# A two-layer attention and retention trunk: preparation steps, bias rows, output-weight squares and projection loads put at other places of the schedule

## The chip, the cores and the metric

The kernel runs on one core of a Trainium2 chip. The metric is the device time of one execution in microseconds (us); smaller is better. The times before are the median, the lowest and the highest of three runs; the profile is of one more execution.

## The reference

Two layers act on x of 2048 tokens by 1024 channels. Each layer normalises x, projects it to eight groups of 512 columns, runs two kinds of heads on them, gates both and projects back.

```python
def hybrid_layer(x, norm_gain, w_in, w_out, rel_bias, cos, sin):
    hn = rms_norm(x, norm_gain)
    proj = hn @ w_in
    aq, ak, av, ag, rq, rk, rv, rg = jnp.split(proj, cuts, axis=-1)
    ya = chunked_rel_attention(aq, ak, av, rel_bias)   # 8 heads x 64, own chunk of 64 and 8 before it
    yr = chunkwise_retention(rq, rk, rv, cos, sin)     # 4 heads x 128, a state carried from chunk to chunk
    y = jnp.concatenate([ya * silu(ag), yr * silu(rg)], axis=-1)
    return x + y @ w_out
```

(The reshapes to heads are left out.) Attention adds a bias for each head by clipped distance and takes a softmax. Retention turns q and k by rotary phases and normalises its output head by head. After the second layer x is normalised once more. All of it is float32.

## The kernel before, in words

**Numbers.** Every float32 operand of a large product is held as two float16 tiles, an upper part and a rest, and each product is three passes of the tensor engine (PE): upper by upper, upper by rest, rest by upper. A weight section of 1024 by 128 is loaded as float32 by `load_sec`, squared and summed by `sumsq` on the scalar engine (ACT), summed over partitions by a small product (`allsum`), and from that a power of two is chosen as a scale. `convert` then makes the upper part on ACT and the rest on the vector engine (DVE). The float32 sections live in pool `w4`, which has three buffers.

**Stages.** A layer has four sections `s`, each with two attention heads and one retention head, and each section has four stages `n` of 512 tokens. A stage has two halves: `dense_T` (projections that come out transposed: queries, keys and their rotary turn) and `dense_V` (values and gates), of 12 rounds each. A round is eight products of 512 columns. The attention and retention of a stage run through the 24 rounds of the next one: `attention` makes one unit (128 queries of one head) in three rounds. In each unit `qk` computes scores, adds the bias and takes the exponential, the SP queue transposes the probabilities (`pT`, L827), and `pv` multiplies by the values two units later. `retention` (L869 products, L873 and L877 operands) goes in between. After the four sections, `wout` projects: for each token tile T of 128 it takes six rounds, in which PE multiplies the transposed, scaled y (tiles `yh`, `yl`) by the output weights, and DVE adds the result to x. It works with later tiles at the same time: y of T + 2 is squared, scaled and split, y of T + 1 is transposed.

**Order.** PE, ACT, DVE and GpSimd (POOL) execute in the order in which the program names their instructions. SyncE (SP), which issues nearly all DMAs, is ordered by a planner, except for issues that `in_turn` or `keep_in_program_order` pins: those stay in program order among themselves. So an issue that isn't pinned may go out long before the step that names it, as soon as its buffer is free.

**Background.** Preparation work is written as generators, put into a list by `push(generator, steps)`. `run` goes through a half stage round by round: it executes what `later(k, ...)` has put off by k rounds, takes one step of attention, and then pulls as many background steps as the remaining steps divided by the remaining rounds, rounded up:

```python
todo = sum(max(b[1], 0) for b in bg)
...
pull(min(-(-todo // max(left, 1)), todo))
left -= 1
```

The rounds that `run` counts on (`thirds`, which becomes `left`) need not be the rounds that there are; steps that are left over run in the next half. `prep_T` and `prep_V` prepare the input weights of the next section, `prep_O` the output weights (`go.os` is their scale), and `prep_Omax` the sum of squares that this scale comes from. `wout_first` takes the first steps of the projection for token tiles 0 and 1 ahead of `wout`: it loads their y and x (`y_load`, `x_load`), squares, scales and splits. `y_turn` transposes a split y by two DMAs into tiles that share buffers with the rotary tables. `bias_scratch` writes two heads' bias rows, repeated 128 times, to DRAM (two DMAs, pinned), and `bias_tiles` reads them back skewed, masks two corners on POOL and scales on ACT.

Of the kernel before, what the change touches and what calls it, by code (L numbers as in the profile page):

```python
# [18 lines left out]
P = 128  # L19
# [8 lines left out]
def hybrid_trunk(ctx: ExitStack, tc: tile.TileContext, x, pos, gain, gcol, w_in, w_out, rel, fgain,  # L28
# [468 lines left out]
    def prep_Omax(l, go):  # L497
        nm = f"O{l}"
        mm = b2.tile([P, 1], F32, tag="omax", name=f"omax{nm}")
        st = load_sec(w_out[l, :, 0:P], f"{nm}m0")  # L500
        for j in range(KT):
            yield
            m1 = sumsq(st, f"{nm}m{j}", None)
            if j + 1 < KT:
                st = load_sec(w_out[l, :, (j + 1) * P:(j + 2) * P], f"{nm}m{j + 1}")
            if j == 0:
                dve.tensor_copy(mm, m1)
            else:
                dve.tensor_tensor(mm, mm, m1, op=ALU.add)
        mm = lowp(mm, nm)  # L510
        for _ in range(4):
            yield
        m = allsum(mm, nm)
        sv, iv = norm_scale(m, nm)
        go.os = b2.tile([P, 1], F32, tag="o_s", name=f"o_s{l}")
        go.oi = b2.tile([P, 1], F32, tag="o_i", name=f"o_i{l}")
        dve.tensor_copy(go.os, sv)
        dve.tensor_copy(go.oi, iv)
        yield
# [87 lines left out]
    def later(k, fn):  # L607
        deferred.append([k, fn])
# [328 lines left out]
    def y_load(l, t):  # L937
        u = St()
        u.nm = f"y{l}_{t}"
        u.t = t  # L940
        if t < 8:
            u.y = w4.tile([P, D], F32, tag="w4", name=f"yy{u.nm}")
        else:
            u.y = b2.tile([P, D], F32, tag="q", name=f"yy{u.nm}")
        sp.dma_start(u.y, y_d[t])
        return u

    def x_load(l, u):
        if l + 1 == DEPTH or u.t < 12:
            f = (hT[l, 0] if l + 1 == DEPTH else hT_of(l + 1, NS - 1))[u.t // 2 % 2].rearrange("p k c -> p (k c)").bitcast(F32)  # L950
            u.x = f[:, u.t % 2 * D:(u.t % 2 + 1) * D]
        else:
            u.x = w4.tile([P, D], F32, tag="w4", name=f"xx{u.nm}")
        sp.dma_start(u.x, x[u.t * P:(u.t + 1) * P, :] if l == 0 else x_d[u.t])

    def y_squares(l, u):
        u.m = b2.tile([P, 1], F32, tag="ym", name=f"ym{u.nm}")
# [100 lines left out]
    def wout_first(l, go, us):  # L1058
        us.append(y_load(l, 0))
        x_load(l, us[0])  # L1060
        us.append(y_load(l, 1))
        u, v = us
        for fns in ((), (lambda: y_squares(l, u),), (lambda: y_scale(u, go),), (lambda: rows_hi(u.rows, u.y, u.sy),),
                    (lambda: rows_lo(u.rows, u.y, u.sy), lambda: y_squares(l, v)), (lambda: y_turn(u), lambda: y_scale(v, go)),
                    (lambda: rows_hi(v.rows, v.y, v.sy),), (lambda: rows_lo(v.rows, v.y, v.sy),)):
            yield
            for fn in fns:
                fn()
        yield

    def wout(l, go, gc, us, wT=None):

# [5 lines left out]
        for r in range(6 * NT):  # L1078
            T, i = divmod(r, 6)
            t, c = halves[r // 3]  # L1080
            u = us[t]
            if ring["att_done"] and i % 3 == 1:
                flow()
            for fn in events.pop(r, ()):
                fn()
            hurry = T + 3 == NT and not end
            if i == 0 and 0 < T < NT - 1 and (end or T + 2 < NT):
                rows_lo(us[T + 1].rows, us[T + 1].y, us[T + 1].sy)
            if (i == 1 and T + 1 < NT and (end or T + 2 < NT)) or (i == 5 and hurry):
                y_turn(us[T + 1 if i == 1 else T + 2])  # L1090
            if i == 0 and T + 2 < NT:
                us.append(y_load(l, T + 2))
            if i == 1 and T + 1 < NT:
                x_load(l, us[T + 1])
            if T + 2 < NT:
                v = us[T + 2]
                if i == 3 - hurry:
                    y_squares(l, v)
                if i == 4 - hurry:
                    y_scale(v, go)  # L1100
                if i == 5 - hurry:
                    rows_hi(v.rows, v.y, v.sy)
                    if hurry:
                        rows_lo(v.rows, v.y, v.sy)
            if i % 3 == 0:
                ps = psD.tile([P, 512], F32, tag="dense", name=f"dO{l}_{t}_{c}")
            for m in range(8 * (i % 3), 8 * (i % 3) + 8):
                kt, w = divmod(m, 3)
                h_, w_ = ((u.h, gc[c].vh), (u.h, gc[c].vl), (u.lo, gc[c].vh))[w]
                pe.matmul(ps, h_[:, kt, :], w_[:, kt, :], start=(m == 0), stop=(m == 23))  # L1110
            if i % 3 == 2:
                xs = u.x[:, c * 512:(c + 1) * 512]
                keep(dve.scalar_tensor_tensor(out=xs, in0=ps, scalar=u.sc[:, 0:1], in1=xs, op0=ALU.mult, op1=ALU.add))
                if end and t + 1 == NT:
                    final_half(t, u.x, c)
                if c == 1:
                    at = lambda k, fn, r=r: events.setdefault(r + k, []).append(fn)
                    if not end:
                        sp.dma_start(x_d[t], u.x)
                        rows = [w_[:, 2 + t % 2].rearrange("p k c -> p (k c)") for w_ in (wT.g.h, wT.g.l)]  # L1120
                        residual(l + 1, t, u.x, at, rows if t < 4 else None, 4 < t < 12 and t % 4 > 0)
                    elif t + 1 < NT:
                        final(t, u.x, at)
            yield
# [251 lines left out]
    for l in range(DEPTH):  # L1376
        gO = [Grp(), Grp()]
        go = Grp()
        for s in range(NSW):
            g = grp(l, s)  # L1380
            for n in range(NS):
# [6 lines left out]
                    st = st0  # L1388
                if n == 0 and not first:
                    bs, bt = bias_scratch(l, s), bias_tiles(l, s, g)  # L1390
                    later(1, lambda bs=bs: next(bs))
                    for k in (6, 10, 17, 21):
                        later(k, lambda bt=bt: next(bt))
                if (l, s) == (0, 0) and 0 < n < NS - 1:
                    if n == 1:
# [15 lines left out]
                        push(prep_O(l, 0, gO[0], go), 9)  # L1411
                if n == NS - 1 and s == 1 and l + 1 < DEPTH:
                    gain_load(l + 1)
                if not first:
                    run(dT, att, 10 if n == 0 else 14 if (l, s, n) == (0, 0, NS - 1) else 22 if (l, s) == (0, 0) else 24)
                if n == NS - 1 and s == NSW - 1:
                    us = []
                    push(wout_first(l, go, us), 10)
                if n == 2 and s == 2:
                    push(prep_Omax(l, go), 13)  # L1420
                if n == NS - 1:
                    if s + 1 < NSW:
                        push(prep_V(l, s + 1, grp(l, s + 1)), 23)
                    else:
                        push(prep_O(l, 1, gO[1], go), 9)
                run(dense_V(l, s, n, g, st), att, 24 if n == NS - 1 and s < NSW - 1 else 12)
                if first:
                    sp_order.__exit__(None, None, None)
# [88 lines left out]
```

## Time and profile before

| what | us |
|---|---|
| median of three runs | 2081.31 |
| lowest and highest run | 2080.66, 2084.20 |
| the profiled execution's own time | 2082.83 |
| its span, first to last instruction | 2081.1 |
| PE busy in the span | 2006.5 |
| DVE, ACT, POOL busy | 1229.8, 1139.5, 683.5 |

The mean granted clock of the tensor engine over the span is 0.991 of full speed. Each row of a view names the line of the kernel, the engine and the tiles as output<-inputs; "idle before" is the time that the engine stood still before an instruction, and the arrow names what released it. In the timeline, the number in square brackets is that idle time. In the chain of waits, a row is a start, a length and what the chain passed through. In a table of windows each row is a stretch (from:to, its length), the busy time of each engine with its number of instructions, the granted clock, the share of time in which the 16 DMA engines were busy, and GB/s. Since every window's DMA share counts packets by their start, it can pass 1.

Layer 0's sections begin near 0, 260, 470 and 678 us, its output projection near 878; layer 1's sections begin near 1072, 1270, 1477 and 1690, its projection near 1895.

### The profile page before, as it was taken

What the parts mean: (1) busy time and instruction counts of PE and PEld (TensorE: products, weight loads), DVE (VectorE), ACT (ScalarE), POOL (GpSimd) and SP (SyncE); (2) the same over time, 40 slices, a digit from 0 to 9 for tenths busy, and PEclk for the clock granted to TensorE, in tenths of its full rate; (3) what the DMA queues carried; (4) which work ended last, traced back from release to release, by engine and by line L of the source; (5) the groups of instructions that cost most, each with busy time, mean ns of one, the idle gap of its engine ahead of it and who ended that gap; (6) DMA issues with size and microseconds to landing.
All of it is one profiled execution on the core that took longest, in us unless ns stands there. A gap on an engine that the chain in (4) does not pass through costs nothing.

```text
span 2081.1 us, 39317 instructions
## 1 busy us (share of the span) xinstructions
PE 2006.5 (96%) x14014; PEld 1052.0 (51%) x14014; DVE 1229.8 (59%) x3817; ACT 1139.5 (55%) x2530; POOL 683.5 (33%) x701
## 2 busy tenths in 40 slices
PE   6988999999999999998999999999999999999998
PEld 4444545555555555544444555555555555554543
DVE  7776556566556555576653556555655565557643
ACT  7566665556565644555443546554655565446432
POOL 0244343444334434430002333444334334343100
PEclk9999999999999999999999999999999999999999
DMA  8678674547484854799765546554755776548874
GB/s 237 162 153 180 142 148 112 114 110 164 117 182 113 167 137 102 153 234 260 203 163 118 125 104 148 120 126 103 152 111 128 178 146 161 127 102 192 211 199 125
DMA packets 645701, 313.63 MB, mean 151 GB/s; under 512 B 459232, under 2 KB 602080, under 8 KB 645504
## 3 DMA queue, kind: packets, MB, share of 16 engines
q1 hardware_dynamic: 645504, 311.12, 65.5%
q8 instruction: 109, 1.79, 0.4%
q14 instruction: 88, 0.72, 0.1%
HBM read 123.26 MB, written 41.98 MB: 79 GB/s over the span
## 4 chain that ended last, share of the span: by engine, by line
PE 49%; DMA 2%; ACT 2%; DVE 1%; issue 0%; SPq 0%; POOL 0%; POOLq 0%; ACTq 0%; DVEq 0%
PE dT L748 15%; PE dV L767 14%; PE dO L1110 13%; PE r L869 2%; DMA pT<-pq 1%; PE S L816 1%; PE S L815 1%; PE o L835 1%; PE o L836 1%; PE o L837 1%; ACT stO1m L312 0%; ACT sc L822 0%; PE ptn L1011 0%; DVE sc L819 0%; ACT pq L824 0%
## 5 line engine op out<-in xcount | busy, mean ns | idle before, releaser
L825 POOL TENSOR_TENSOR pq<-sc,pq 128x640 f16<-128x640 f32 (+4 forms) x256 | 319.6, 1248 | 872.1 <-ACT pq L824 460.2
L822 ACT ACTIVATE sc<-sc,mq,cT 128x640 f32<-128x640 f32 (+4 forms) x256 | 218.4, 853 | 629.4 <-DVE rl L841 338.3
L767 PE MATMUL dV<-whV,hTh 128*128 128x512 f16 x1024 | 353.1, 381 | 4.3 <-DVE gt L785 4.2
L767 PE MATMUL dV<-wlV,hTh 128*128 128x512 f16 x1024 | 353.2, 381 | 0.0
L767 PE MATMUL dV<-whV,hTl 128*128 128x512 f16 x1024 | 353.1, 380 | 0.0
L748 PE MATMUL dT<-hTh,whT 128*128 128x512 f16 x1008 | 349.2, 382 | 2.1 <-DMA hTh<-xa 1.1
L748 PE MATMUL dT<-hTh,wlT 128*128 128x512 f16 x1008 | 348.0, 380 | 0.0
L748 PE MATMUL dT<-hTl,whT 128*128 128x512 f16 x1008 | 347.8, 380 | 0.0
L767 PEld LDWEIGHTS <-hTh 128*128 128x128 f16 x2048 | 196.8, 98 | 219.2 <-DVE gt L785 6.5
L748 PEld LDWEIGHTS <-whT 128*128 128x128 f16 x2016 | 193.0, 98 | 214.9 <-issue 10.6
L819 DVE CUSTOM_DVE_ANT_0 sc<-S,bias 128x640 f32<-128x640 f32 (+4 forms) x256 | 188.3, 736 | 112.7 <-PE S L816 111.3
L1110 PE MATMUL dO<-whO,yly 128*128 128x512 f16 x512 | 194.6, 380 | 1.5 <-DMA yly<-hTl 0.8
L1110 PE MATMUL dO<-whO,yhy 128*128 128x512 f16 x512 | 194.8, 381 | 1.0 <-DMA yhy<-hTh 1.0
L1110 PE MATMUL dO<-wlO,yhy 128*128 128x512 f16 x512 | 194.8, 380 | 0.0
L824 ACT ACTIVATE pq<-sc 128x640 f16<-128x640 f32 (+4 forms) x256 | 171.5, 670 | 8.1
L1110 PEld LDWEIGHTS <-yhy 128*128 128x128 f16 x1024 | 99.9, 98 | 116.1 <-DMA yhy<-hTh 1.5
L767 PEld LDWEIGHTS <-hTl 128*128 128x128 f16 x1024 | 99.3, 98 | 110.6 <-issue 1.9
L748 PEld LDWEIGHTS <-wlT 128*128 128x128 f16 x1008 | 97.5, 98 | 113.1 <-issue 6.2
L815 PE MATMUL S<-k,q 128*128 128x128 f16 (+3 forms) x592 | 142.9, 268 | 0.2
L835 PE MATMUL o<-v,pT 128*128 128x65 f16 x1120 | 130.0, 194 | 12.3 <-DMA pT<-pq 12.3
L836 PE MATMUL o<-v,pT 128*128 128x64 f16 x1120 | 130.2, 195 | 0.0
L816 PE MATMUL S<-k,q 128*128 128x128 f16 (+3 forms) x592 | 130.2, 268 | 0.0
(352 smaller groups left out, 3462.1 us busy)
## 6 DMA issues: line engine op xcount, KB each, us to landing
q<-qq SPq DMA_DIRECT2D x128, 128.0 KB, 2.4
yyy<-y_d SPq DMA_DIRECT2D x32, 512.0 KB, 4.7
stT<-in_w_in_dram SPq DMA_DIRECT2D x27, 512.0 KB, 5.1
stV<-in_w_in_dram SPq DMA_DIRECT2D x26, 512.0 KB, 4.7
k<-kk SPq DMA_DIRECT2D x128, 64.0 KB, 2.0
swp<-rot SPq DMA_DIRECT2D x64, 128.0 KB, 2.7
tabc<-tab SPq DMA_DIRECT2D x32, 256.0 KB, 3.0
tabs<-tab SPq DMA_DIRECT2D x32, 256.0 KB, 3.2
```

The costliest lines, as they stand in the source:

```text
L748: pe.matmul(ps, w_[:, j, kt, :], h_[:, kt, :], start=(m == 0), stop=(m == 23))
L767: pe.matmul(ps, h_[:, kt, a * P:(a + 1) * P], w_[:, kt, :], start=(m == 0), stop=(m == 23))
L815: pe.matmul(o, st.q[:, hx, 0, cs], k_, start=True, stop=False)
L816: pe.matmul(o, st.q[:, hx, 1, cs], k_, start=False, stop=True)
L819: dve.tensor_tensor_reduce(out=v, in0=S[:, 0:w], in1=g.bias[hx][:, 640 - w:640], scale=1.0, scalar=-3.0e38, op0=ALU.add, op1=ALU.max, accu ...
L822: act.activation(v, v, AF.Exp, bias=m[:, 0:1], scale=g.c[:, 0:1])
L824: act.activation(pq[:, 0:w], v, AF.Copy)
L825: pool.tensor_tensor(pq[:, w:2 * w], v, pq[:, 0:w], op=ALU.subtract)
L835: pe.matmul(o[:, 0:65], u.p[:, b, :], v_[:, 0:65], start=(b == 0), stop=False)
L836: pe.matmul(o[:, 0:64], u.p[:, b, :], v_[:, 65:129], start=False, stop=False)
L869: pe.matmul(out_, w_, m_, start=(i == 0), stop=(i + 1 == len(pairs)))
L1110: pe.matmul(ps, h_[:, kt, :], w_[:, kt, :], start=(m == 0), stop=(m == 23))
```

## The change

Five edits. (1) In the last stage of layer 0's first section, the divisor of `dense_T`'s run goes from 14 to 18, which spreads the 25 steps of section 1's `prep_T`. (2) At the start of a section, `bias_scratch` runs in the third round instead of the first, and the first two steps of `bias_tiles` in rounds 7 and 11 instead of 6 and 10. (3) `prep_Omax` is pushed before `dense_T` of stage 2 of section 2 instead of before its `dense_V`, with 21 steps instead of 13; it has two sections loaded or loading at a time. (4) `wout_first` is pushed before `dense_T` of a layer's last stage, with a divisor of 12, instead of before `dense_V`; it no longer transposes tile 0, which `with_turn` does in the eighth of its rounds beside `prep_O`. (5) y loads from tile 2 and x loads from tile 1 on are pinned, and y of tile T + 3 is loaded in round 3 of tile T instead of in round 0 of tile T + 1.

```diff
     def prep_Omax(l, go):
         nm = f"O{l}"
         mm = b2.tile([P, 1], F32, tag="omax", name=f"omax{nm}")
-        st = load_sec(w_out[l, :, 0:P], f"{nm}m0")
+        load = lambda j: load_sec(w_out[l, :, j * P:(j + 1) * P], f"{nm}m{j}")
+        for _ in range(4):
+            yield
+        sts = [load(0), load(1)]
+        for _ in range(4):
+            yield
         for j in range(KT):
             yield
-            m1 = sumsq(st, f"{nm}m{j}", None)
-            if j + 1 < KT:
-                st = load_sec(w_out[l, :, (j + 1) * P:(j + 2) * P], f"{nm}m{j + 1}")
+            m1 = sumsq(sts[j], f"{nm}m{j}", None)
+            if j + 2 < KT:
+                sts.append(load(j + 2))
...
-        sp.dma_start(u.y, y_d[t])
+        i = sp.dma_start(u.y, y_d[t])
+        if t > 1:
+            in_turn(i)
         return u
...
-        sp.dma_start(u.x, x[u.t * P:(u.t + 1) * P, :] if l == 0 else x_d[u.t])
+        i = sp.dma_start(u.x, x[u.t * P:(u.t + 1) * P, :] if l == 0 else x_d[u.t])
+        if u.t:
+            in_turn(i)
...
-                    (lambda: rows_lo(u.rows, u.y, u.sy), lambda: y_squares(l, v)), (lambda: y_turn(u), lambda: y_scale(v, go)),
+                    (lambda: rows_lo(u.rows, u.y, u.sy), lambda: y_squares(l, v)), (lambda: y_scale(v, go),),
...
+    def with_turn(gen, us):
+
+        for r in range(12):
+            if r == 7:
+                y_turn(us[0])
+            next(gen, None)
+            yield
...
-            if i == 0 and T + 2 < NT:
-                us.append(y_load(l, T + 2))
+            if r == 0 or (i == 3 and T + 3 < NT):
+                us.append(y_load(l, T + 3 if r else 2))
...
-                    later(1, lambda bs=bs: next(bs))
-                    for k in (6, 10, 17, 21):
+                    later(3, lambda bs=bs: next(bs))
+                    for k in (7, 11, 17, 21):
                         later(k, lambda bt=bt: next(bt))
...
+                if n == 2 and s == 2:
+                    push(prep_Omax(l, go), 21)
+                last = n == NS - 1 and s == NSW - 1
+                if last:
+                    us = []
+                    push(wout_first(l, go, us), 9)
                 if not first:
-                    run(dT, att, 10 if n == 0 else 14 if (l, s, n) == (0, 0, NS - 1) else 22 if (l, s) == (0, 0) else 24)
-                if n == NS - 1 and s == NSW - 1:
-                    us = []
-                    push(wout_first(l, go, us), 10)
-                if n == 2 and s == 2:
-                    push(prep_Omax(l, go), 13)
+                    run(dT, att, 12 if last else 10 if n == 0 else 18 if (l, s, n) == (0, 0, NS - 1) else 22 if (l, s) == (0, 0) else 24)
                 if n == NS - 1:
                     if s + 1 < NSW:
                         push(prep_V(l, s + 1, grp(l, s + 1)), 23)
                     else:
-                        push(prep_O(l, 1, gO[1], go), 9)
+                        push(with_turn(prep_O(l, 1, gO[1], go), us), 12)
```

## The prediction

> **What bounds the kernel now.** I read the page first, then the waits of PE, then a table of windows over the stretches that the diff touches, then single rows.
>
> ```profile
> span 2081.1 us, 39317 instructions
> ## 1 busy us (share of the span) xinstructions
> PE 2006.5 (96%) x14014; PEld 1052.0 (51%) x14014; DVE 1229.8 (59%) x3817; ACT 1139.5 (55%) x2530; POOL 683.5 (33%) x701
> ```
> PE is busy for all but 74.6 us; no other engine passes 59%. The change adds and removes no matmul, so it can win only inside those 74.6 us and in PE's clock. Who ends PE's idle time:
> ```profile
> PE o L835 <- DMA pT<-pq: 12.3, 11, 2.1
> PE r L869 <- DVE dT L877: 8.1, 9, 2.1
> PE r L869 <- DVE sh L877: 8.1, 5, 4.2
> PE msg L326 <- DVE mbg L319: 5.0, 1, 5.0
> PE r L869 <- ACT dT L873: 4.3, 3, 1.5
> ```
> Two families: the transposed probabilities (pT) arrive late from the SP queue, and retention's small products (r) come before ACT and DVE have made their operands (dT, sh). Where they lie (stretch, length, PE, PEld, DVE, ACT, POOL busy, granted clock, DMA share, GB/s):
> ```profile
> 195.00:235.00 40.00, 36.43 (x285) 19.71 (x286) 22.69 (x81) 26.38 (x57) 13.28 (x12) 1.00 0.75 169
> 1270.00:1297.00 27.00, 25.59 (x200) 13.64 (x199) 16.73 (x59) 16.38 (x39) 5.92 (x8) 1.00 0.80 188
> 1477.00:1503.00 26.00, 24.12 (x173) 12.20 (x170) 15.34 (x52) 16.01 (x37) 5.60 (x7) 0.93 0.92 193
> 570.00:595.00 25.00, 25.00 (x196) 13.61 (x194) 12.44 (x40) 12.42 (x26) 9.41 (x9) 1.00 0.69 148
> 595.00:620.00 25.00, 22.60 (x171) 11.92 (x170) 15.41 (x52) 19.25 (x47) 10.09 (x10) 1.00 0.91 217
> 1611.00:1636.00 25.00, 22.60 (x164) 11.81 (x163) 14.67 (x52) 19.14 (x46) 8.77 (x8) 0.94 0.89 223
> 849.00:878.00 29.00, 26.71 (x209) 14.53 (x207) 18.82 (x56) 18.89 (x40) 15.36 (x13) 1.00 0.61 139
> 1866.00:1895.00 29.00, 26.70 (x206) 14.48 (x205) 19.39 (x56) 18.73 (x40) 15.39 (x13) 1.00 0.67 129
> 878.00:936.00 58.00, 54.30 (x404) 28.75 (x402) 40.39 (x115) 31.17 (x61) 17.85 (x15) 0.97 1.03 231
> 936.00:980.00 44.00, 38.51 (x199) 17.87 (x198) 26.71 (x70) 23.37 (x43) 3.60 (x5) 0.96 1.11 259
> 980.00:1071.00 91.00, 91.00 (x445) 43.76 (x444) 52.57 (x110) 40.71 (x70) 4.40 (x8) 1.00 0.78 199
> 1895.00:1910.00 15.00, 13.34 (x100) 6.72 (x98) 11.35 (x36) 8.95 (x19) 3.36 (x3) 1.00 1.10 295
> 878.71:882.12 3.41, 3.41 (x23) 1.73 (x21) 1.62 (x4) 3.38 (x7) 1.40 (x1) 0.50 1.07 260
> 974.28:977.69 3.41, 3.35 (x12) 2.31 (x13) 3.20 (x14) 2.73 (x4) 0.00 (x0) 0.50 1.02 281
> 1493.11:1496.52 3.41, 3.41 (x9) 1.22 (x8) 1.47 (x8) 2.32 (x7) 0.59 (x1) 0.50 0.91 227
> 1633.05:1636.46 3.41, 3.02 (x12) 1.37 (x13) 1.80 (x8) 2.02 (x5) 0.28 (x1) 0.50 1.36 309
> 616.60:620.00 3.40, 2.49 (x20) 1.37 (x21) 2.78 (x12) 1.04 (x2) 0.55 (x1) 1.00 0.98 251
> ```
> Length less PE's busy time is what a stretch has to give. 570:595 and 980:1071 are quiet neighbours with no idle time. The last five rows come back below.
>
> **The change part by part.** The profiled execution took 2082.8 us, 1.7 more than its span and 1.5 above the median of the three timed runs (2081.3); I sum against the first and carry the difference over to the median.
>
> *(a) First preparation of section 1.* The last stage of section 0 (from 195 us) gives its 25 steps 18 divisor rounds instead of 14. Worked by the rule in run(): with 14, two steps fall in each of eleven rounds; with 18, two in each of seven rounds and then one. Square and scale of a weight section are three steps apart, so at two a round the sum on PE comes one round after the square on ACT:
> ```profile
> 218.51 0.16 PE L326 MATMUL msT<-mbT,ones 128*128 128x1 bf16 x1 [1.70 <-DVE mbT L319]
> ```
> This is the third section; the first two fall in the seven unchanged rounds and keep their share of the stretch's 3.57 us. The third gets three rounds and its 1.70 should go. The fourth section's steps slip into the projection after it, again two rounds from square to sum as before, and by its fifth round both schedules are at the same step. Gain 1.7; bounds 0 and 3.4.
>
> *(b) Bias rows.* At the start of a section with n = 0 two broadcast writes go out, now two rounds later; the first two bias-tile steps go one round later (a load, or two POOL memsets and an ACT copy), and those have a whole stage until L819 reads them, so I cost them at nothing. The writes now stand:
> ```profile
> 1273.85 1.17 SPq L567 DMA_DIRECT2D toep<-rel_d  x2
> 1275.12 0.53 SPq L297 DMA_DIRECT2D stT<-in_w_in_dram  x1
> 1276.19 4.97 SPq L827 DMA_TRANSPOSE pT<-pq  x1
> ```
> ```profile
> DMA to landing us min/median/max: 2.3/3.0/9.4
> ```
> ```profile
> 1276.19 8.93 DMA pT<-pq
> 1285.13 0.04 issue
> 1285.17 0.20 PE o L835
> ```
> The second fence is over all pT transposes, the third the chain of waits. A transpose that takes 3.0 us in the median took 8.93 behind three large transfers, and PE began its products the moment it landed. The stretch's idle time is 27.00 - 25.59 = 1.41 us here and 26.00 - 24.12 = 1.88 in the next section. Two rounds later the writes follow this transpose. The next one follows three rounds after it: an attention unit is three rounds, and the next unit's L835 starts 1291.56 - 1285.17 = 6.4 us on, so a round is 2.1 us.
> ```profile
> 1291.56 0.19 PE L835 MATMUL o<-v,pT 128*128 128x65 f16 x1
> ```
> The writes would go out near 1278, land like today's in 5 to 6.4 us, and the next transpose, issued near 1285 behind them and the q copies, has till about 1290. Its 3.0 us fit, narrowly. Gain 1.41 + 1.88 = 3.3; bounds 0 (the stall moves one unit on) and 3.3.
>
> *(c) Squares of the output weights.* Eight squares on ACT today run in the projection half of stage 2, section 2; the generator now starts with the transposed half, loads two ahead, and puts three squares there and five in the first five rounds of the other half.
> ```profile
> L312 ACT ACTIVATE stO0m<-stO0m x8: 1039/1042/1058, 595.0 to 614.2; 128x1024 f32<-128x1024 f32 x8
> ```
> ```profile
> 616.64 0.29 PE L869 MATMUL r<-rv,dT 128*128 128x128 f16 x2 [1.53 <-ACT dT L873]
> ```
> ACT is 19.25 of 25 us busy there and 12.42 of 25 just before. PE idles 2.40 us in layer 0 and 2.40 in layer 1 (595:620 and 1611:1636). Moving three squares of 1.04 us levels ACT at about 15.5 and 16.1, and the last rounds, where PE waits, have no square left. Against that: 18.89 of 29 us at 849:878 is the same share, and PE waits there too. I take 3.6 of 4.8; bounds 0 and 4.8. The loads go out earlier into a DMA share of 0.69; that hides them.
>
> *(d) First steps of the output projection.* wout_first (two squares, two scalings and two splits of y) ran with prep_O's second half in one projection phase: 19 steps in 12 rounds, two a round at first. Now its nine steps take nine of the 12 rounds before, the prep_O steps go one a round, and the transposes of the first y tile come at the eighth. ACT is left with four of its eight 128x1024 steps in 849:878. At about 1.04 us each that takes 18.89 to 14.7 of 29, the share of the quiet row 570:595. Idle: 2.29 and 2.30 us; they include a trailing 0.1 that stays. Gain 4.4; bounds 0 and 4.6. What is late next: the transposes of the first y tile, whose rows are now ready a half stage early; they need only land before the first output product.
>
> *(e) Loads of the projection pinned in program order.* y of tile T+3 is asked for three rounds earlier than before, but y and x loads may no longer be drawn ahead on SP.
> ```profile
> L945 SPq DMA_DIRECT2D yyy<-y_d x32: 319/565/1742, 751.8 to 2036.0; - x32
> ```
> ```profile
> L954 SPq DMA_DIRECT2D xxy<-in_x_dram x4: 333/459/593, 952.3 to 1051.0; - x4
> ```
> ```profile
> DVE hTh L1006 <- DMA x_d<-hTh: 5.1, 1, 5.1
> ```
> ```profile
> 974.34 0.48 PE L1011 MATMUL ptn<-ident,hTh 128*128 128x128 f32 x1 [2.31 <-DVE ymy L966]
> ```
> The x tiles 12 to 15 (xxy) are fetched from 952 us on, in a stretch with DMA share 1.11, though the projection asks for them after 1000 us, where the share is 0.78. There a store that DVE waits 5.1 us for sits in a full SP queue, and PE stands 2.31. Idle time: 3.70 (878:936), 5.49 (936:980) and 1.66 (1895:1910), together 10.85. Pinning takes loads out of 936:980 but moves no bytes away from 878:936, and layer 1's x tiles, fetched early today, come into 1895:1910. I take half, 5.4; bounds -4 and 10.8. The loads keep about six rounds before their use, more than 12 us at 2.1 a round.
>
> Waits removed: 1.7 + 3.3 + 3.6 + 4.4 + 5.4 = 18.4. New waits: the pT waits above are eleven of up to 2.1 us each; I charge two such, 4.2, for transfers that now meet another transpose. Net 14.2.
>
> *The clock.* In four of the touched places a stretch of 3.41 us at clock 0.50 begins within 3 us of a stall (878.71, 974.28, 1493.11, 1633.05), and matmul work that would take 1.7 us takes 3.4. The equal stall of 2.40 before 618 us leaves the clock at 1.00 (616.60:620.00), so where it falls decides. If two of the four go and a new wait brings one, 1.7 more. The Trainium skill (TensorE: Matmul & The Clock Gate, Part 1) says that an idle window of some 3.4 us, free-running, halves the clock, and advises against idle gaps over that length; by that rule gaps of 2.4 us cost no clock, and the sum would stay at 14.2. The rows here show halving after shorter ones, so I go by the rows.
>
> Sum: 14.2 + 1.7 = 15.9; 2082.8 - 15.9 = 2066.9, by the median **2065.4, say 2065**.
>
> **The rivals.** *Stalls move, they don't go.* The bias writes meet the next transpose, ACT's lag meets retention's product six rounds earlier, (e) gives nothing: 1.7 + 4.4 remain, 2075. For it: the narrow fit in (b), the equal ACT share in (c). The Trainium skill (DMA: Bandwidth & Descriptors, Queues, rings and completion order) has each engine consume a ring's descriptors in order, so bytes moved past one transpose stand before the next; that is this rival's mechanism, and no run here yet shows the next one late.
> *The order is not what the diff writes.* SP's unpinned issues are placed by a planner: the first y load goes out at 751.8, some 125 us before its products. If SP's order stays much as it is and the level of ACT matters less than I think: 2081, no change.
> *Slower.* In the five tiles of each layer that run beside attention, every y and x load now stands at a fixed place in SP's line, in front of a transpose that PE waits for. By (b), three large transfers cost a transpose 8.93 - 3.0 = 5.9 us, about 2.0 each; two loads by five tiles by two layers are 40 us of added latency. Without (e) the other parts gain 15.9 - 5.4 = 10.5; from the point where more than 10.5 of the 40 reaches PE the kernel is slower, and 15 give 2081.3 - 10.5 + 15 = 2086. Against: today's loads stand before transposes too, at worse places.
>
> **How the numbers follow.** About 0.2% (4.2 us) is what a measurement of this kernel can tell. Chances: forecast 0.60 (its own range 2054 to 2072), stalls move 0.17, no change 0.09, slower 0.14. Everything removed, 25.2 us and the four clock stretches, gives 2081.3 - 25.2 - 6.8 = 2049; 2053 is low enough. The upper end, 2082, takes in the first two rivals and leaves out the slower one. Faster 0.76, same 0.10, slower 0.14.
>
> **What would show it.** Right: 595:620's counterpart without idle time at its end; no 1.20 and 1.01 before the first output product; pT near 3 to 5 us at the start of sections 1 and 2 of layer 1; xxy loads after 1000 us; fewer rows at clock 0.50. Wrong: L835 waits of 2 us one unit further on; L1110 waiting for yhy or yly tile after tile; DVE L1113 waiting for an x load.

## The result, and the profile after

The changed kernel takes 2064.71 us (median of four runs, 2061.84 to 2066.02) where the kernel before takes 2080.98 (four runs, 2078.07 to 2084.20): a ratio of 0.992 [0.9901, 0.9938]. In another set of runs the same two kernels stood at 2062.35 and 2079.75, 0.9916 [0.9899, 0.9932]. The code of the changed kernel has moved a little: L827, L835, L869, L873, L877, L945, L954 and L1110 of before are L832, L840, L874, L878, L882, L950, L961 and L1127 now.

The page of the profile after (its execution took 2061.84 us, the lowest of the four):

```profile
span 2060.0 us, 39310 instructions
PE 1997.9 (97%) x14014; PEld 1049.6 (51%) x14014; DVE 1231.2 (60%) x3817; ACT 1137.7 (55%) x2530; POOL 687.9 (33%) x701
```

The same 14014 matmuls. PE (busy time, share, instructions) is idle for 62.1 us where it was 74.6, and its busy time is 8.6 us shorter with the same work: that second part can't come from waits. From the list of PE's waits after (in all us, how many, the longest):

```profile
PE r L874 <- DVE dT L882: 8.6, 11, 2.1
PE dV L772 <- DVE gt L790: 6.4, 5, 3.3
PE o L840 <- DMA pT<-pq: 6.0, 6, 2.4
```

The late transposes have halved, from 12.3 us in eleven waits to 6.0 in six. The wait on ACT's dT (4.3 in three) is gone; the wait on DVE's dT has grown from 8.1 to 8.6, and that of the projections (dV) on DVE's gate operand gt from 4.2 in two to 6.4 in five. By place (stretch, length, PE, PEld, DVE, ACT, POOL busy, granted clock, DMA share, GB/s), after:

```profile
195.00:243.00 48.00, 44.28 (x346) 24.04 (x347) 26.96 (x99) 30.91 (x67) 18.40 (x16) 1.00 0.72 160
284.00:294.00 10.00, 10.00 (x71) 5.19 (x69) 6.28 (x22) 5.72 (x15) 6.59 (x9) 1.00 0.74 152
1259.00:1286.00 27.00, 27.00 (x218) 14.63 (x216) 18.21 (x62) 17.04 (x39) 5.56 (x6) 1.00 0.89 196
1464.00:1490.00 26.00, 26.00 (x202) 14.04 (x201) 17.32 (x58) 16.46 (x38) 5.31 (x5) 1.00 0.87 199
591.00:616.00 25.00, 23.50 (x184) 12.44 (x183) 15.59 (x55) 17.66 (x42) 9.05 (x8) 1.00 0.99 216
1594.00:1619.00 25.00, 23.56 (x173) 12.24 (x172) 15.31 (x55) 17.37 (x42) 9.04 (x8) 1.00 0.95 218
843.00:872.00 29.00, 27.74 (x219) 15.37 (x218) 19.46 (x46) 17.26 (x38) 16.01 (x13) 1.00 0.83 168
1847.00:1876.00 29.00, 27.47 (x218) 15.19 (x216) 19.98 (x47) 16.78 (x37) 16.02 (x13) 1.00 0.85 161
872.00:930.00 58.00, 54.43 (x410) 28.50 (x407) 38.08 (x119) 32.17 (x62) 18.21 (x16) 1.00 0.99 209
930.00:974.00 44.00, 41.18 (x214) 19.27 (x215) 29.02 (x68) 23.86 (x46) 3.77 (x6) 0.96 1.10 256
1876.00:1891.00 15.00, 15.00 (x122) 8.06 (x121) 10.26 (x35) 9.30 (x19) 4.75 (x4) 1.00 0.83 205
932.72:936.13 3.41, 3.41 (x10) 1.24 (x9) 1.94 (x6) 2.47 (x6) 0.55 (x1) 0.50 1.23 222
```

and four stretches of before that were not shown (the last two hold a whole pair of touched places each):

```profile
195.00:243.00 48.00, 44.42 (x347) 24.14 (x348) 27.03 (x99) 30.89 (x67) 17.25 (x16) 1.00 0.70 157
284.00:294.00 10.00, 7.97 (x49) 3.80 (x47) 6.58 (x21) 4.71 (x12) 6.15 (x7) 0.88 0.99 151
849.00:975.00 126.00, 114.52 (x788) 58.45 (x786) 82.01 (x229) 68.64 (x134) 36.81 (x33) 0.98 0.96 221
1866.00:1910.00 44.00, 40.04 (x304) 21.20 (x303) 30.74 (x91) 27.68 (x59) 18.75 (x16) 1.00 0.82 186
```

Length less PE's busy time, before to after: first preparation 3.58 to 3.72; start of the sections of layer 1 1.41 and 1.88 to 0 and 0; the same place in layer 0 (284:294) 2.03 to 0; squares 2.40 and 2.40 to 1.50 and 1.44; first steps of the projection 2.29 and 2.30 to 1.26 and 1.53; projection 10.85 to 3.57 + 2.82 + 0 = 6.39. In the last row the clock is at half. It is the only such stretch after 250 us, apart from the last 4 us, which stand at half clock in both executions; before had five there, the four of the prediction and one at 291.6. Over the whole execution, that end left out, the half-clock time went from 34.0 us to 13.6.

### The profile page after: what moved, and what is told of

It reads as the page before. It is cut to its first block, busy times and chain, and to the rows that moved or that the text cites. A ratio compares the mean times of both kernels' runs of the same rounds, so it can differ in the third digit from the quotient of the medians.

```text
span 2060.0 us, 39310 instructions
## 1 busy us (share of the span) xinstructions
PE 1997.9 (97%) x14014; PEld 1049.6 (51%) x14014; DVE 1231.2 (60%) x3817; ACT 1137.7 (55%) x2530; POOL 687.9 (33%) x701
## 5 line engine op out<-in xcount | busy, mean ns | idle before, releaser
L827 ACT ACTIVATE sc<-sc,mq,cT 128x640 f32<-128x640 f32 (+4 forms) x256 | 218.4, 853 | 615.7 <-DVE rl L846 298.3
L1127 PE MATMUL dO<-whO,yly 128*128 128x512 f16 x512 | 194.7, 380 | 1.4 <-DMA yly<-hTl 1.4
L1127 PE MATMUL dO<-wlO,yhy 128*128 128x512 f16 x512 | 194.8, 380 | 0.0
L1127 PE MATMUL dO<-whO,yhy 128*128 128x512 f16 x512 | 194.7, 380 | 0.0
L1127 PEld LDWEIGHTS <-yhy 128*128 128x128 f16 x1024 | 100.0, 98 | 115.1 <-issue 1.4
L840 PE MATMUL o<-v,pT 128*128 128x65 f16 x1120 | 129.4, 193 | 6.0 <-DMA pT<-pq 6.0
```

The costliest lines, as they stand in the source:

```text
L827: act.activation(v, v, AF.Exp, bias=m[:, 0:1], scale=g.c[:, 0:1])
L840: pe.matmul(o[:, 0:65], u.p[:, b, :], v_[:, 0:65], start=(b == 0), stop=False)
```

## The experiments

The theory, T: each part works where the prediction put it, by taking a wait off PE, and the parts add up. The rivals: a stall only moves one unit or one section on; or a part gives nothing and another does its work.

**Each part alone, on the kernel before** (before: 2079.85 us in these runs).

*Bias rows alone.*

```diff
-                    later(1, lambda bs=bs: next(bs))
-                    for k in (6, 10, 17, 21):
+                    later(3, lambda bs=bs: next(bs))
+                    for k in (7, 11, 17, 21):
```

> Before with only the bias rows later. If the broadcast writes hold up the transpose behind them, PE's idle time of 1.41 us near 1285 and of 1.88 us near 1492 goes, and with the second of them the half-clock stretch at 1493: 3.3 to 5.0 us less than before, near 2077. If the 2.03 us near 291 belongs to this part as well (it is gone in the changed kernel), up to 3.7 us more (2.03 and a half-clock stretch of 1.7). Rival: the writes only meet the next transpose; L835 then waits 1 to 2 us one unit later and the time stays within 1 us of before.

Measured: 2075.81 us, 0.9984 [0.9973, 0.9994]. Its windows at the starts of section 1 of layer 0 and of sections 1 and 2 of layer 1:

```profile
284.00:294.00 10.00, 10.00 (x71) 5.24 (x70) 6.14 (x21) 5.53 (x15) 6.77 (x9) 1.00 0.72 154
1266.00:1293.00 27.00, 27.00 (x213) 14.66 (x212) 16.34 (x56) 17.58 (x43) 6.69 (x6) 1.00 0.80 183
1471.00:1497.00 26.00, 26.00 (x203) 14.04 (x202) 15.81 (x56) 17.15 (x42) 6.69 (x6) 1.00 0.85 186
```

All three stalls go with this edit alone, the one at 291 us that the prediction didn't count too. The stall doesn't come back one unit later: the next wait on a transpose in these sections is one of 0.43 us at 1506.

*Squares of the output weights alone* (the new `prep_Omax`, and its push):

```diff
+                if n == 2 and s == 2:
+                    push(prep_Omax(l, go), 21)
...
-                if n == 2 and s == 2:
-                    push(prep_Omax(l, go), 13)
```

> Before with only the squares of the output weights spread over both halves. If ACT's backlog is what PE waits for, the two stalls of 2.40 us (near 617 and 1633) shrink to the 1.2 to 1.4 us that the changed kernel shows there, and the half-clock stretch at 1633 goes: 2 to 4 us less than before, near 2078. Rival: the loads, not the squares, matter, since they fill the DMA engines near 600; then pT waits change in that place and not retention's.

Measured: 2077.20 us, 0.9991 [0.9982, 1.0]. The waits of PE between 582 and 620 us:

```profile
PE dV L772 <- DVE gt L790: 0.6, 1, 0.6
PE r L874 <- DVE dT L882: 0.6, 1, 0.6
```

The 1.53 behind ACT is gone, two waits of 0.6 on DVE are next. The idle time of the place is 1.33 here and 1.50 in the whole change, so this part stands by itself, and it gives about half of what it was after. The time alone wouldn't tell: its interval reaches 1.

*First steps of the projection alone.*

```diff
-                if n == NS - 1 and s == NSW - 1:
+                last = n == NS - 1 and s == NSW - 1
+                if last:
                     us = []
-                    push(wout_first(l, go, us), 10)
+                    push(wout_first(l, go, us), 9)
...
-                        push(prep_O(l, 1, gO[1], go), 9)
+                        push(with_turn(prep_O(l, 1, gO[1], go), us), 12)
```

(with the new `with_turn`, the shorter `wout_first` and the divisor of 12, as in the whole change).

> Before with only the first projection steps moved a half stage ahead and the first transposes of y in the eighth round. If ACT's load at the end of the last half is the cause, the stalls of 2.21 us before the first output product shrink by 0.7 to 1.0 us in each layer, and the half-clock stretch at 879 goes: 2 to 4 us less than before. Rival: the transposed y tiles that are ready earlier change the order on the SP queue, and the waits on pT and yly between 889 and 962 change as well, by more than 2 us in sum.

Measured: 2079.61 us, 0.9999 [0.999, 1.0007]: nothing.

*Pinned loads alone.*

```diff
-        sp.dma_start(u.y, y_d[t])
+        i = sp.dma_start(u.y, y_d[t])
+        if t > 1:
+            in_turn(i)
...
-            if i == 0 and T + 2 < NT:
-                us.append(y_load(l, T + 2))
+            if r == 0 or (i == 3 and T + 3 < NT):
+                us.append(y_load(l, T + 3 if r else 2))
```

(and x likewise).

> Before with only the projection's x and y loads pinned and y asked for three rounds earlier. If loads drawn ahead by the planner are what fills the SP queue, PE's idle time between 880 and 980 falls from 9.2 us to about 6.4 as in the changed kernel, layer 1's 1.67 us at 1897 and 1905 goes, and the half-clock stretch at 974 with its 2.31 us stall goes: 4 to 6 us less than before. Rival: pinning alone moves stalls from one transpose to another, and the projection keeps 8 us or more of idle time; the gain there in the changed kernel then comes from the first steps being done earlier.

Measured: 2078.71 us, 0.9992 [0.9983, 1.0001]: 1.1 us, hardly more than nothing. The four parts alone give 4.0, 2.7, 0.2 and 1.1 us, 8.1 of the 16.3, and the fifth, the first preparation, has yet to be placed. Either the first preparation is worth 8 us, or two of the parts need each other.

**The two projection parts together**, on the kernel before (2079.75 us in these runs): both edits above.

> Before with the first projection steps and the pinned loads together, nothing else. Alone the two gave a ratio of 0.9999 and 0.9992, and each alone left 9.1 us or more of PE's idle time in the two projections' first 100 us (11.4 + 2.7 us with the first steps, 7.1 + 2.7 with the loads). If they need each other (early first steps free the buffers of w4, which the planner then fills with y loads unless they are pinned), both together show about 6.4 + 0 us there, as the changed kernel does, and some 6 to 9 us less than before in time. Rival: the parts simply add, and the rest of the change's 16 us comes from elsewhere: 1 to 2 us less than before, with 9 us or more of idle time left in the projections.

Measured: 2069.30 us, 0.9949 [0.9934, 0.9965]: 10.4 us, where the two alone gave 0.2 and 1.1. Now the sum fits: 4.0 + 2.7 + 10.4 = 17.1, beside 17.4 of the whole change in this set of runs. The same places in the three kernels, first steps alone:

```profile
849.00:975.00 126.00, 114.21 (x791) 57.70 (x788) 77.87 (x211) 64.73 (x128) 37.49 (x33) 0.99 0.96 217
1866.00:1910.00 44.00, 40.00 (x299) 21.27 (x297) 27.70 (x79) 24.84 (x53) 19.20 (x16) 0.96 0.77 174
```

pinned loads alone:

```profile
849.00:975.00 126.00, 116.63 (x807) 59.67 (x806) 83.48 (x235) 70.56 (x136) 37.43 (x33) 0.99 0.93 208
1858.00:1902.00 44.00, 38.99 (x291) 20.56 (x290) 26.75 (x79) 27.36 (x58) 19.41 (x16) 0.96 0.79 164
```

and both:

```profile
849.00:975.00 126.00, 118.92 (x820) 60.64 (x818) 84.95 (x229) 71.10 (x141) 37.08 (x34) 1.00 0.97 220
1852.00:1896.00 44.00, 41.31 (x315) 22.06 (x314) 27.48 (x80) 26.12 (x57) 19.59 (x17) 1.00 0.88 176
```

Idle time of PE, the two stretches added: before 11.48 + 3.96 = 15.4, first steps alone 15.8, loads alone 14.4, both 9.8. So 5.6 us of the 10.4 are idle time here. And with both, no half-clock time falls into these stretches, where first steps alone, loads alone and before each have two such beginning in them. In the first of the two stretches the first steps alone take PE's waits on retention's operands from 2.2 us to 0.6, but its waits on pT go from 4.3 to 7.1; with both, the waits on pT are 3.4. The reason for the longest of these waits stands in SP's queue. First steps alone, the queue about 880 us, a row being the start, the time that the issue took and what was issued:

```profile
879.37 0.46 SPq L945 DMA_DIRECT2D yyy<-y_d  x1
879.92 0.38 SPq L928 DMA_DIRECT2D y_d<-yr  x1
880.39 0.38 SPq L945 DMA_DIRECT2D yyy<-y_d  x1
880.87 1.39 SPq L704 DMA_TRANSPOSE kt<-rot  x1
882.35 4.75 SPq L827 DMA_TRANSPOSE pT<-pq  x1
```

```profile
889.10 0.20 PE L835 MATMUL o<-v,pT 128*128 128x65 f16 x1 [2.80 <-DMA pT<-pq]
```

Both parts, the same place:

```profile
878.80 0.38 SPq L303 DMA_DIRECT2D stT<-in_w_in_dram  x1
879.28 1.40 SPq L704 DMA_TRANSPOSE kt<-rot  x1
880.77 0.59 SPq L850 DMA_DIRECT2D y_d<-ya  x1
881.46 1.49 SPq L827 DMA_TRANSPOSE pT<-pq  x1
```

With the first steps half a stage earlier, their float32 tiles come free half a stage earlier, and the unpinned y loads of 512 KB are drawn ahead into the free buffers: four within 11 us (869.7, 871.8, 879.4, 880.4; the kernel before has its four from 877.7 on), the last two right in front of a transpose of pT, which lands 6.70 us after it was issued at 882.35. PE waits 2.80 for it. With the loads pinned the next y load comes only at 886.4, the transpose issued at 881.46 lands after 3.53, and nobody waits. Pinning gives back what the first steps alone would lose; pinning alone has little to mend, since the buffers come free late anyway. This is read from one wait of layer 0; the others weren't followed one by one. The loads-alone kernel holds two changes, the pins and the y load three rounds earlier; which of the two matters isn't known.

**The first preparation undone**, on the changed kernel (before: 2079.40 us in these runs).

```diff
-18 if (l, s, n) == (0, 0, NS - 1)
+14 if (l, s, n) == (0, 0, NS - 1)
```

(a piece of the line with `run(dT, ...)`).

> The changed kernel with the divisor of the first preparation set back from 18 to 14. The trace of the changed kernel has lost the wait of 1.70 us at 218 but has two new ones, 0.56 at 230 and 1.25 at 241. If part (a) only moves its wait, setting it back changes the time by less than 1 us, gives the 1.70 back and takes the two new ones away. Rival: it also moved loads on the SP queue and with them the 2.03 us near 291 of the kernel before; then that wait returns, with 2 to 4 us.

Measured: 2062.97 us, 0.993 [0.9913, 0.9947], the time of the changed kernel. The first preparation is worth nothing. The changed kernel's timeline of PE shows why:

```profile
230.47 0.16 PE L326 MATMUL msT<-mbT,ones 128*128 128x1 bf16 x1 [0.56 <-DVE mbT L319]
...
241.50 0.16 PE L326 MATMUL msV<-mbV,ones 128*128 128x1 bf16 x1 [1.25 <-DVE mbV L319]
```

The 1.70 at 218.51 is gone; 0.56 at the last of the four T sections and 1.25 at the first V section have come, 1.81 in all. With the divisor set back, the 1.70 is there again (at 219.03) and these two are not.

**The squares moved further**, on the changed kernel, in two ways. All earlier by four rounds, seven of the eight in the transposed half:

```diff
-        for _ in range(4):
-            yield
         sts = [load(0), load(1)]
...
-                    push(prep_Omax(l, go), 21)
+                    push(prep_Omax(l, go), 17)
```

> The changed kernel with the squares of the output weights four rounds earlier still, so that seven of eight fall into the transposed half, where ACT is busy half of the time. If ACT's backlog in the second half is what is left of those stalls, the 1.39 us near 598 to 614 and the 1.21 us near 1610 to 1617 fall below 0.5 each: about 2 us less than the changed kernel. Rival: ACT is not short there but late by its own chain of exponentials; then the waits stay, or new ones come in the transposed half.

Measured: 2070.03 us, 0.9962 [0.9947, 0.9976], 6 to 10 us more than the other three kernels of these runs. My reason for trying it, that the fewer squares stand in the second half the better, fell. PE's timeline, and ACT's:

```profile
589.81 0.23 PE L872 MATMUL r<-rv,dT 128*128 128x128 f16 x1 [2.64 <-DVE dT L880]
```

```profile
587.94 1.06 ACT L312 ACTIVATE stO0m<-stO0m 128x1024 f32<-128x1024 f32 x1 [4.26 <-DMA stO0m<-in_w_out_dram]
```

The fault isn't ACT's busy share but its order: a square stood 4.26 us waiting for its own weights (issued at 581.98, landed at 587.91), DVE behind it waited for the square's sum, and PE for DVE. Four rounds earlier this section wasn't there yet. So, at a square a round, the three squares that the change puts in the transposed half are near what the loads allow.

Slower, a square every second round:

```diff
             yield
+            if j:
+                yield
             m1 = sumsq(sts[j], f"{nm}m{j}", None)
...
-                    push(prep_Omax(l, go), 21)
+                    push(prep_Omax(l, go), 24)
```

> The changed kernel with one square in every second round over both halves instead of one in each of eight rounds. If ACT falls behind because a square a round is more than it has room for, wherever they stand (four rounds earlier only moved the stall to 590 and 1597, with 2.4 to 2.6 us), half the rate leaves no stall above 0.5 us in these two stages: 2 to 4 us less than the changed kernel. Rival: any square that falls between retention's first product and its operand delays it; then stalls of 0.5 to 1 us appear at several places and the sum stays near 1.5 us a layer.

Measured: 2063.48 us, 0.992 [0.9905, 0.9936], as the changed kernel beside it (2062.35). Its idle time at the place is 1.52 in layer 0 and 2.26 in layer 1: no square is late, but small waits on DVE and on a transpose take their place.

**Half of the output preparation moved with the first steps**, so that `with_turn` runs a half stage earlier:

```diff
                     push(wout_first(l, go, us), 9)
+                    push(with_turn(prep_O(l, 1, gO[1], go), us), 12)
                 if not first:
-                    run(dT, att, 12 if last else
+                    run(dT, att, 24 if last else
```

(the push before `dense_V` goes, and the transposes come in the tenth of its rounds, not the eighth; the expectation names the seventh).

> The changed kernel with the second half of the output weights also started in the transposed half of the last stage, so that its last split on ACT comes three rounds earlier, and with the transposes of the first y tile in the seventh round. If the splits near the end of the half are what is left of the stall before the first output product, 1.26 us at 872 and 1.53 at 1875 fall below 0.5: about 2 us less than the changed kernel. Rival: the stall there is the chain of retention itself, and stays.

Measured: 2060.20 us, 0.9909 [0.9892, 0.9927]. Its windows:

```profile
843.00:872.00 29.00, 29.00 (x226) 15.81 (x224) 18.89 (x52) 18.68 (x40) 15.43 (x13) 1.00 0.89 195
1847.00:1876.00 29.00, 29.00 (x239) 16.24 (x237) 19.17 (x51) 17.84 (x39) 15.05 (x13) 1.00 0.85 176
```

The 1.26 and 1.53 us that the changed kernel still waits there are gone, though ACT is busier (18.68 of 29 us against 17.26). So the level of ACT wasn't what PE waited on; the wait goes with the order of the steps. DVE's rows in the changed kernel show which step it was:

```profile
869.82 1.28 DVE L336 SCALAR_TENSOR_TENSOR wlO<-stO,o_s,whO 128x1024 f16<-128x1024 f32 x1
...
871.28 0.28 DVE L882 SCALAR_TENSOR_TENSOR dT<-dT,r 128x128 f16<-128x128 f16 x1
```

The split of an output-weight section, 1.28 us on DVE, stands in front of retention's dT, which PE waits for until 871.61; in layer 1 the same split stands at 1873.58. With the preparation half a stage earlier, no split stands there: DVE makes dT at 869.37.

*The slower squares and this together.*

> The slower squares and the earlier second half of the output weights, both on the changed kernel. If they are independent, their gains add: 4 to 8 us less than the changed kernel, near 2058, with no idle time above 0.5 us in the stages with squares and in the last stage of each layer. Rival: the output weights' loads and the longer list of squares get in each other's way through the three buffers of w4, and the sum is no better than the earlier output weights alone.

Measured: 2059.09 us, 0.9901 [0.9885, 0.9916], the lowest of all. The places of the first steps hold 0.07 us or less of idle time, those of the squares 2.9 and 2.2, more than in the changed kernel. Beside the changed kernel in the same runs (0.9916 [0.9899, 0.9932]) the intervals overlap: that this version beats it by the 3 us of the medians isn't settled, and neither is the gain of the version above.

**The next section's weight loads pinned too**, on the changed kernel, for a wait of 2.45 us in its profile:

```profile
924.55 0.57 SPq L961 DMA_DIRECT2D hTh<-in_x_dram  x1
925.22 2.32 SPq L832 DMA_TRANSPOSE pT<-pq  x1
```

```profile
931.96 0.20 PE L840 MATMUL o<-v,pT 128*128 128x65 f16 x1 [2.45 <-DMA pT<-pq]
```

The transpose that PE waits for is the one issued at 925.22: it lands at 931.91, 6.69 us later. In front of it stands an x load. The loads that the expectation blames (two y tiles, a weight section and the mask) are issued from 927.60 on, behind it. In the kernel before, the same order (x load, transpose at 933.20) gave 5.27 us and a wait of 0.83.

```diff
-            sp.dma_start(st[i], v[:, i * h:(i + 1) * h, :])
+            in_turn(sp.dma_start(st[i], v[:, i * h:(i + 1) * h, :]))
```

> The changed kernel with the loads of the next layer's first weight sections pinned too, in layer 0's projection. If weights drawn ahead on the SP queue are what still delays pT there (a wait of 2.45 us at 932, behind two y tiles, a weight section and the mask, and a half-clock stretch with it), that wait goes: 2 to 4 us less than the changed kernel, with nothing lost later. Rival: the weights are then late for their squares, and the next layer's preparation or its first products wait; no gain, or up to 5 us lost near 1050.

Measured: 2064.19 us, 0.9931 [0.9914, 0.9947]: no gain. The wait shrinks to 1.34 us (at 932.97), but the idle time of the projection is 6.6 us against 6.39; other waits took its place. That the pins shrink it isn't shown either: the next profile, of the changed kernel as it is, doesn't have the 2.45.

**The changed kernel again**, as a second profile.

> The changed kernel once more, to stand beside the others on one chip: near 0.992 of before, with PE's idle time by stage within 0.7 us of its first profile after the first 200 us, and half-clock stretches at places that differ from its first profile's, if the clock's windows run free of the program.

Measured: 2062.35 us, 0.9916 [0.9899, 0.9932]. PE's idle time repeats within about 1 us (63.1 in all, 62.1 in the first), but not every wait of the projection does: the 2.45 at 931.96 isn't there, and an earlier transpose is waited for 2.11 until 916.62 (0.93 at that place in the first). The half-clock stretch after 250 us begins at 917.3 here, not at 932.7.

## Why the prediction was right, and where its steps were off

Forecast: 14.2 us of waits and 1.7 of clock. The two profiled executions differ by 21.1 us of span: 12.5 of idle time and 8.6 of PE's busy time, which goes with the clock (below). The medians differ by 16.3, since the profile of before lies 1.9 above its median and the profile after 2.9 below. So the forecast of the time held, and the make-up of the sum less well; that the total came so close is partly luck. (a), (c), (d) and (e) gave 7.0 us less than forecast, and a charge for new waits that was too high, a wait at 291 us that wasn't counted and a larger gain of clock made up for it. Of the signs named, two didn't come: the stage with the squares still waits 0.57 us near its end, and other waits took the place of the 1.20 and 1.01 before the first output product.

*(a)* 1.7 forecast, -0.1 measured, and no time lost when it is undone. The step that failed is the last: "the fourth section's steps slip into the projection after it, again two rounds from square to sum as before". They slip, but with V's steps behind them at two a round, and the waits came there. The stall moved one section on.

*(b)* 3.3 forecast; 3.3 went at the two places (0.29 came elsewhere in the second one's stage), and 2.0 more at 284:294. In layer 1 the order is as worked out, the transpose first and then the writes:

```profile
1263.01 0.38 SPq L297 DMA_DIRECT2D stT<-in_w_in_dram  x1
1265.13 1.26 SPq L832 DMA_TRANSPOSE pT<-pq  x1
1266.45 1.22 SPq L572 DMA_DIRECT2D toep<-rel_d  x2
...
1271.49 1.99 SPq L832 DMA_TRANSPOSE pT<-pq  x1
```

The transposes land in 3.0 to 5.0 us here instead of 8.93. The wait at 291 us in layer 0, which the prediction doesn't have, is another matter. The writes of that section are issued at 256.92 and 257.81 in the kernel before and have landed by 263; in front of the transpose stands a weight load:

```profile
280.44 2.38 SPq L297 DMA_DIRECT2D stT<-in_w_in_dram  x2
284.50 1.73 SPq L827 DMA_TRANSPOSE pT<-pq  x1
```

With the bias edit alone the order here is the same, but the second weight load lands after 5.03 us instead of 7.19 and the transpose after 3.98 instead of 6.24. All five profiles without the bias edit have a wait at this place (0.69 to 2.03 us), the nine with it none above 0.21. So this gain belongs to the edit, which also moves two steps of `bias_tiles` by a round, but how it comes about isn't shown.

*(c)* 3.6 forecast, 1.9 measured. The mechanism was right (the wait behind ACT's square went), the size off: with ACT levelled, DVE's operands are next (0.6 us a wait in the experiment).

*(d)* 4.4 forecast, 1.8 measured. The argument was ACT's share of the stretch, 14.7 of 29 us; it came to 17.26 and 16.78. The experiment with `prep_O` beside it has a higher share and no wait, so the share was the wrong measure: what is waited for is a split of 1.28 us on DVE, which the prediction doesn't count.

*(e)* 5.4 forecast, as half of what was there; 4.5 measured. The x tiles are fetched from 1012.8 us on, and DVE's wait of 5.1 for the store in a full queue is down to 2.1. But it is a gain of (d) and (e) together. The forecast added them as separate terms, and for (d) named the transposes as what comes late next; what came next in fact was the y loads of (e), drawn ahead into the buffers that (d) frees. That (e) would pin them is why the sum still held.

*New waits.* 4.2 charged; by these terms (-0.1 + 3.3 + 2.0 + 1.9 + 1.8 + 4.5 = 13.4) against 12.5 in all, about 0.9 came elsewhere. Of that, PE's idle time before 195 us, where no edit works, grew from 34.9 us to 36.0, with a wait of 1.60 for gt at 67.82. The wait of 2.45 at 932, 0.83 before, lies inside (e)'s 4.5.

*The clock.* 1.7 forecast, some 8 measured between the two profiles and some 4 over all runs. I let two of four stretches go and one come; all four went, that at 291.6 too, and one came at 932.7. The rest of the 20.4 us of half clock that is missing lies in the first 250 us, which the change hardly touches. Over the fourteen profiled executions, PE's busy time runs with the time at half clock, from 1996.7 us with 10.2 to 2006.5 with 34.0, and single ones lie up to 2 us off that line: 9.8 for 23.8, or 1.4 us for each stretch of 3.41. By that the 20.4 us are 8.4 of the 8.6. About half of that is the luck of these two executions: the mean granted clock is 0.9937 over the 49 runs of the kernel before that list it, and the profile of before, at 0.991, is at their lowest; over the eight runs of the changed kernel it is 0.9960. A difference of 0.0023 over some 2070 us is 9.5 us at half clock, an estimated 3.9 us of time, about what the medians leave after the idle time (16.3 - 12.5).

*The rivals.* Stalls move: true of (a), and in small of (c), not of (b). The order isn't what the diff writes: true of the first steps alone, where unpinned loads spoiled it, not of the whole. Slower by loads in front of transposes: at 932 us an x load stands in front of a late transpose, with 2.45 us of wait and a half-clock stretch behind it. But the same order was there before, with 0.83, and not every execution pays it; the price is 1.6 us, not the 15 that the rival needed.

## What to carry to other kernels

Where transfers are placed by a planner, a step that frees a buffer earlier also lets the next unpinned load out earlier: look at which transfer that is and which short one it will stand in front of, and change both together. Try the parts alone before believing that they add up; here two parts worth 0.2 and 1.1 us were worth 10.4 together. And a spread of preparation that moves one wait should be followed to the end of its list of steps, since what is spread less at the front is packed at the back.

## What the runs showed of the hardware

A wait of about 2 us of PE can cost another 1.4 us by the clock, and whether it does varies from one execution to the next. Before 195 us, where no edit works, all fourteen profiles hold the same waits, of the same or nearly the same length. After the one of 2.07 us near 95 us, a stretch of 3.41 us at half clock begins within 1.2 us in six profiles and not in the other eight; the changed kernel, profiled twice, is once among the six and once among the eight. Around the end of the wait of 2.55 us near 43 us such a stretch begins in eight of the fourteen, of the 3.26 near 185 us in ten, and of the one of 3.6 to 4.5 near 109 us in all. The two stretches at 932.7 and 917.3 each stand right behind the longest wait of their own projection (2.45 and 2.11). By the Trainium skill (TensorE: Matmul & The Clock Gate, Part 1), an idle window of some 3.4 us is what halves the clock; the waits of 2.07, 2.55 and 3.26 us named here are shorter, so the trace doesn't agree.

A transpose in SP's queue lands later behind large transfers: at nearly the same place it landed 3.53 us after its issue with a weight load as the last large one in front of it, and 6.70 with two y loads there. The Trainium skill (DMA: Bandwidth & Descriptors, Queues, rings and completion order) says that a ring's descriptors are taken in order, and these two numbers agree with it. The queue's order isn't all of it: behind an x load, the transpose that PE waits for near 932 us took 5.27 us before, 6.69 in the changed kernel and 5.36 with the weight loads pinned. Why isn't shown.
